# Row normalisation by the sum of absolute values: transfers moved to the software queue in a fixed order, each engine's share as a single packet

## The chip, the cores and the metric

The kernel runs on one core of one Trainium2 chip. The metric is the device time in microseconds (us). A ratio is the mean time of one kernel's fast runs over that of the other kernel's fast runs of the same rounds, so it is not quite the ratio of the medians that are quoted.

## The reference

```python
# x: (32, 512, 1024) float32
sums = np.sum(np.abs(x), axis=-1, keepdims=True)
return (x / (sums + 1e-8)).astype(np.float32)
```

That is 16,384 rows of 1,024 floats. 67.1 MB are read and 67.1 MB written.

## The kernel before

There are 8 tiles of 128 partitions x 16 rows x 1,024 floats, 8 MB each, and 3 buffers. Each tile is loaded by one transfer, worked on in place and stored, all on the hardware queue that SyncE issues. In the profiles DVE is VectorE, ACT is ScalarE, and Pool is GpSimd. DVE reduces the rows and takes the reciprocals. DVE then scales 10 of the 16 rows one by one, and ACT scales the other 6. The last two tiles are worked on and stored in chunks of 4 rows.

```python
def process_chunk(x_tile, out_ap, r0, rN, mv):
    s = stats.tile([P, rN], mybir.dt.float32, tag="s")
    nc.vector.tensor_reduce(out=s[:, :], in_=x_tile[:, r0 : r0 + rN, :], ...)   # cut: axis X, add, absolute value
    inv = stats.tile([P, rN], mybir.dt.float32, tag="inv")
    nc.vector.reciprocal(out=inv[:, :], in_=s[:, :])
    for r in range(rN):
        if r < mv:
            nc.vector.tensor_scalar_mul(...)        # cut: row r0 + r times inv[:, r]
        else:
            nc.scalar.activation(..., func=Copy, scale=inv[:, r : r + 1])
    nc.sync.dma_start(out=out_ap[:, r0 : r0 + rN, :], in_=x_tile[:, r0 : r0 + rN, :])

MV = 10
for i in range(ntiles):
    x_tile = sbuf.tile([P, R, d], x.dtype)          # R = 16, 3 buffers
    nc.sync.dma_start(out=x_tile[:, :, :], in_=x_t[i, :, :, :])
    if i < ntiles - 2:
        process_chunk(x_tile, out_t[i], 0, R, MV)
    else:
        C = 4
        for c0 in range(0, R, C):
            process_chunk(x_tile, out_t[i], c0, C, (MV * C) // R)
```

The compiler orders the instructions of each engine itself. On the queue the order became, with L for a load and S for a store: L0 L1 L2 S0 S1 S2 L3 L4 L5 S3 S4 S5 L6 L7, then S6 and S7 in four chunks each.

## Time and profile before

| | before |
|---|---|
| time, median of the first 3 runs | 318.28 us (318.22 to 318.55) |
| span of the profiled execution | 316.9 us |
| DVE busy / ACT busy | 60% / 18% |
| hardware queue, share of 16 engines' span | 98.6% |
| mean rate | 424 GB/s |

These lines are from the profile page of before: busy time by engine, the mean busy share of the 16 DMA engines in 40 slices of the span (in tenths), and the queue.

```profile
span 316.9 us, 261 instructions
...
DVE 190.8 (60%) x104; ACT 56.7 (18%) x53; POOL 0.2 (0%) x4
...
DMA  9999999999999999999999999999999999999797
...
q1 hardware_dynamic: 3168, 134.22, 98.6%
```

The DMA engines bound the kernel. They are busy in every slice, while DVE is idle 40% of the time. The view of waits gives DVE's idle time (line, what it waited for, us in total, times, longest):

```profile
DVE s L37 <- DMA x_tile<-in_x_dram: 111.2, 3, 44.6
```

DVE waits 111 us for loads, but the DMA engines are busy during those waits, with stores and then with the awaited loads, so this idle time costs nothing by itself.

The table of windows shows one place where the DMA engines do stop. The columns are the window, its length, busy time of DVE, ACT and POOL with instruction counts, the granted clock, the DMA share and GB/s.

```profile
286.00:293.00 7.00, 7.00 (x4) 2.19 (x2) 0.00 (x0) 1.00 1.01 433
293.00:295.00 2.00, 2.00 (x5) 0.85 (x1) 0.00 (x0) 1.00 0.58 246
295.00:299.00 4.00, 4.00 (x2) 3.41 (x4) 0.00 (x0) 1.00 1.00 422
299.00:301.00 2.00, 2.00 (x4) 0.00 (x0) 0.00 (x0) 1.00 0.62 262
```

At 294 and at 300 us the engines run dry, because DVE finishes the last tile's chunks late: it reduces the second chunk before it has scaled the first. Below, a stretch in which an engine has no packet to move is called a dry spot.

The trace also records every DMA packet, and when each of the 16 engines reports its share of a transfer as landed. From those records:

- A 64 KB packet takes 2.418 us at the median, which is 434 GB/s over 16 engines. An engine moves 8 such packets for an 8 MB transfer, 19.34 us.
- The records do not name the engine. I joined packets end to start into 16 chains. All figures "per engine" below are per chain.

### The profile page before, as it was taken

The numbers are of one execution on the slowest core, as the hardware profiler recorded it, in microseconds if no ns is written. First come the engines' busy times: TensorE is split into PE (matmuls) and PEld (weight loads), VectorE is DVE, ScalarE is ACT, GpSimd is POOL, SyncE is SP. The second block draws the span as 40 slices with busy tenths as digits, with TensorE's granted clock in tenths as the row PEclk, the third lists the DMA queues.
The fourth block names the chain that finished last, engine by engine and source line by source line (L and its number), as shares of the span: only waits on it lengthen the run. The fifth ranks groups of instructions, "written<-read, shape, count | busy, mean of one in ns | idle before, by whom it ended". The sixth has DMA issues, their size and how long they took to land.

```text
span 316.9 us, 261 instructions
## 1 busy us (share of the span) xinstructions
DVE 190.8 (60%) x104; ACT 56.7 (18%) x53; POOL 0.2 (0%) x4
## 2 busy tenths in 40 slices
DVE  0019999999990000039999999980000069999910
ACT  0010080080080000000160070080000002522520
POOL 0000000000000000000000000000000000000000
DMA  9999999999999999999999999999999999999797
GB/s 397 397 397 513 414 397 397 397 438 488 397 397 505 422 397 397 521 405 397 480 447 397 397 489 438 397 430 480 414 397 480 438 405 422 399 431 432 335 430 331
DMA packets 3170, 134.24 MB, mean 424 GB/s; under 512 B 352, under 2 KB 352, under 8 KB 352
## 3 DMA queue, kind: packets, MB, share of 16 engines
q1 hardware_dynamic: 3168, 134.22, 98.6%
q14 instruction: 2, 0.02, 0.0%
HBM read 67.11 MB, written 67.11 MB: 424 GB/s over the span
## 4 chain that ended last, share of the span: by engine, by line
DVE 57%; DMA 35%; issue 4%; ACT 0%; ACTq 0%; SPq 0%; DVEq 0%
DVE s L37 41%; DMA x_tile<-in_x_dram 35%; DVE x_tile L48 15%; DVE inv L45 1%; ACT x_tile L54 0%; ACTq L99 0%; SPq L60 0%; DVEq L45 0%; DVEq L48 0%
## 5 line engine op out<-in xcount | busy, mean ns | idle before, releaser
L37 DVE TENSOR_REDUCE s<-x_tile 128x4 f32<-128x4096 f32 (+1 forms) x14 | 138.3, 9891 | 111.2 <-DMA x_tile<-in_x_dram 111.2
L54 ACT ACTIVATE x_tile<-x_tile,inv 128x1024 f32<-128x1024 f32 x52 | 55.4, 1137 | 223.9 <-DVE inv L45 223.9
L48 DVE TENSOR_SCALAR x_tile<-x_tile,inv 128x1024 f32<-128x1024 f32 x76 | 51.4, 748 | 0.3
L54 ACT ACT_TABLE_LOAD x1 | 1.3, 1283 | 22.8 <-DMA x_tile<-in_x_dram 22.8
L45 DVE RECIPROCAL inv<-s 128x4 f32<-128x4 f32 (+1 forms) x14 | 2.6, 200 | 0.4
L88 POOL MEMSET const-bfloat16-1.0<- 128x1 bf16 x1 | 0.1, 101 | 0.0
L88 POOL MEMSET const-uint8-127<- 128x1 uint8 x1 | 0.1, 101 | 0.0
L88 POOL MEMSET const-float32-0.0<- 128x1 f32 x1 | 0.1, 98 | 0.2 <-issue 0.2
L88 POOL MEMSET const-float32-1.0<- 128x1 f32 x1 | 0.1, 98 | 0.0
## 6 DMA issues: line engine op xcount, KB each, us to landing
out_dram<-x_tile SPq DMA_DIRECT2D x8, 2048.0 KB, 9.9
x_tile<-in_x_dram SPq DMA_DIRECT2D x8, 51.0
out_dram<-x_tile SPq DMA_DIRECT2D x6, 29.5
```

Source lines behind the costliest of these rows:

```text
L37: nc.vector.tensor_reduce(out=s[:, :], in_=x_tile[:, r0 : r0 + rN, :], axis=mybir.AxisListType.X, op=mybir.AluOpType.add, apply_absolute_v ...
L45: nc.vector.reciprocal(out=inv[:, :], in_=s[:, :])
L48: nc.vector.tensor_scalar_mul(out=x_tile[:, r0 + r, :], in0=x_tile[:, r0 + r, :], scalar1=inv[:, r : r + 1],)
L54: nc.scalar.activation(out=x_tile[:, r0 + r, :], in_=x_tile[:, r0 + r, :], func=mybir.ActivationFunctionType.Copy, scale=inv[:, r : r + 1],)
L88: nc = _bacc.Bacc("TRN2", target_bir_lowering=False, num_devices=1)
```

## The change

The intent is to keep the DMA engines fed without a break. The first three loads stay on the hardware queue. Everything later goes to the software queue, which Pool issues, in one fixed order in which loads and stores alternate. Each engine's share of a transfer is asked for as a single packet. On the compute side, DVE scales half of the rows in one two-input multiply and ACT scales the other half, and only the last tile is split, into two halves.

```diff
+        nc.vector.tensor_scalar_add(out=s[:, :k], in0=s[:, :k], scalar1=EPS)
+        nc.vector.tensor_mul(out=x_tile[:, r0 : r0 + kv, :], in0=x_tile[:, r0 : r0 + kv, :],
+            in1=inv[:, :kv].unsqueeze(2).to_broadcast([P, kv, d]))          # kv = half of the rows
-            if r < mv:
-                nc.vector.tensor_scalar_mul(...)
 ...
+    def span(i):
+        k = R // 2 if i == ntiles - 1 else R
+        return [(r0, k) for r0 in range(0, R, k)]
 ...
+            (nc.sync if i < BUFS else nc.gpsimd).dma_start(
+                out=x_tile[:, r0 : r0 + k, :], in_=x_t[i][:, r0 : r0 + k, :], single_packet=True)
 ...
+            nc.gpsimd.dma_start(
+                out=out_t[i][:, r0 : r0 + k, :], in_=tiles[i][:, r0 : r0 + k, :], single_packet=True)
 ...
+    plan = [("L", i) for i in range(BUFS)]
+    for i in range(ntiles):
+        plan.append(("S", i))
+        nxt = i + BUFS - 1
+        if BUFS <= nxt < ntiles:
+            plan.append(("L", nxt))
+    last = max(k for k, p in enumerate(plan) if p[0] == "L")
+    plan[last - 1], plan[last] = plan[last], plan[last - 1]
+    with tc.manual_schedule():      # every engine keeps the program's order
 ...
```

The order is L0 L1 L2 S0 S1 L3 S2 L4 S3 L5 S4 L6 L7 S5 S6 S7, with L7 and S7 in two halves.

More of the change, by code (lines that the diff above doesn't have):

```diff
@@ L7 @@
 from concourse._compat import with_exitstack
+FP32 = mybir.dt.float32
+EPS = 1e-8
 @with_exitstack
@@ L26, with normalize @@
     ntiles = n // (P * R)
+    BUFS = 3
     x_t = x_flat.rearrange("(n p r) d -> n p r d", p=P, r=R)
     out_t = out_flat.rearrange("(n p r) d -> n p r d", p=P, r=R)
-    BUFS = 3
     sbuf = ctx.enter_context(tc.tile_pool(name="sbuf", bufs=BUFS))
-    stats = ctx.enter_context(tc.tile_pool(name="stats", bufs=BUFS))
-    def process_chunk(x_tile, out_ap, r0, rN, mv):
-        s = stats.tile([P, rN], mybir.dt.float32, tag="s")
+    stats = ctx.enter_context(tc.tile_pool(name="stats", bufs=4))
+    def normalize(x_tile, r0, k, kv):
+        s = stats.tile([P, R], FP32)
         nc.vector.tensor_reduce(
-            out=s[:, :],
-            in_=x_tile[:, r0 : r0 + rN, :],
+            out=s[:, :k],
+            in_=x_tile[:, r0 : r0 + k, :],
             axis=mybir.AxisListType.X,
@@ L43, in process_chunk @@
         )
-        inv = stats.tile([P, rN], mybir.dt.float32, tag="inv")
-        nc.vector.reciprocal(out=inv[:, :], in_=s[:, :])
-        for r in range(rN):
-            if r < mv:
-                nc.vector.tensor_scalar_mul(
-                    out=x_tile[:, r0 + r, :],
-                    in0=x_tile[:, r0 + r, :],
-                    scalar1=inv[:, r : r + 1],
-                )
-            else:
-                nc.scalar.activation(
-                    out=x_tile[:, r0 + r, :],
-                    in_=x_tile[:, r0 + r, :],
-                    func=mybir.ActivationFunctionType.Copy,
-                    scale=inv[:, r : r + 1],
-                )
@@ L60, in process_chunk @@
-        nc.sync.dma_start(out=out_ap[:, r0 : r0 + rN, :], in_=x_tile[:, r0 : r0 + rN, :])
-    MV = 10
-    for i in range(ntiles):
-        x_tile = sbuf.tile([P, R, d], x.dtype)
-        nc.sync.dma_start(out=x_tile[:, :, :], in_=x_t[i, :, :, :])
-        if i < ntiles - 2:
-            process_chunk(x_tile, out_t[i], 0, R, MV)
-        else:
-            C = 4
-            for c0 in range(0, R, C):
-                process_chunk(x_tile, out_t[i], c0, C, (MV * C) // R)
+        nc.vector.tensor_scalar_add(out=s[:, :k], in0=s[:, :k], scalar1=EPS)
@@ new lines, in normalize @@
+        inv = stats.tile([P, R], FP32)
+        nc.vector.reciprocal(out=inv[:, :k], in_=s[:, :k])
+        nc.vector.tensor_mul(
+            out=x_tile[:, r0 : r0 + kv, :],
+            in0=x_tile[:, r0 : r0 + kv, :],
+            in1=inv[:, :kv].unsqueeze(2).to_broadcast([P, kv, d]),
+        )
+        for r in range(kv, k):
+            row = x_tile[:, r0 + r, :]
+            nc.scalar.activation(
+                out=row,
+                in_=row,
+                func=mybir.ActivationFunctionType.Copy,
+                scale=inv[:, r : r + 1],
+            )
@@ new lines, in span, with load @@
+    def span(i):
+        k = R // 2 if i == ntiles - 1 else R
+        return [(r0, k) for r0 in range(0, R, k)]
+    tiles = {}
+    def load(i):
+        x_tile = sbuf.tile([P, R, d], FP32)
+        tiles[i] = x_tile
+        for r0, k in span(i):
+            (nc.sync if i < BUFS else nc.gpsimd).dma_start(
+                out=x_tile[:, r0 : r0 + k, :], in_=x_t[i][:, r0 : r0 + k, :], single_packet=True
+            )
+        for r0, k in span(i):
+            normalize(x_tile, r0, k, k // 2)
@@ new lines, in store @@
+    def store(i):
+        for r0, k in span(i):
+            nc.gpsimd.dma_start(
+                out=out_t[i][:, r0 : r0 + k, :], in_=tiles[i][:, r0 : r0 + k, :], single_packet=True
+            )
+    plan = [("L", i) for i in range(BUFS)]
[6 more added lines that the diff above has]
+    plan[last - 1], plan[last] = plan[last], plan[last - 1]
@@ L77 @@
+    with tc.manual_schedule():
+        for what, i in plan:
+            if what == "L":
+                load(i)
+            else:
+                store(i)
 _INS = ['x']
```

## The prediction

> **What bounds the kernel now.** The 16 DMA engines. The page's queue part gives the hardware queue 98.6% of 16 engines' span; its slices show DMA at 9 in 39 of 40; the mean is 424 GB/s. DVE is busy 60%, ACT 18%. The chain of waits names DVE reduces (41%), which misleads: DVE sits idle twice for about 44 us waiting for loads (timeline), but the DMA engines are writing stores then. All transfers run one after another on one queue. In the trace's DMA packets a 64 KB packet takes 2.418 us at the median, so an 8 MB transfer (8 per engine) takes 19.34 us, and transfers land 19.3 to 19.8 us apart: 434 GB/s. The Trainium skill ("DMA: Bandwidth & Descriptors", Where 436 GB/s comes from) puts the ceiling at 435; the trace agrees.
>
> **Where slack is left.** Sixteen transfers make 309.5 us. The rest of the 316.9 us span is about 2.9 us before the stream runs at rate, 0.9 us from the last landing to the end, and about 3.5 us of losses: roughly 1.2 us where load 2 meets store 0 (the packets at 58 us take 3.4 to 3.8 us), about 0.5 us at 236, and about 2 us near the end, where the engines run dry at 294 and 300 us because the last tile's chunks finish late on DVE.
>
> **What the change does.** Bytes, buffers and DMA engines stay. Per tile it adds a tiny add (about 0.2 us, like the reciprocal's 0.20) and multiplies 8 rows in one two-input instruction in place of 10 single-row ones (6.7 us). The reduce runs at 1.05 ns an element; the skill ("VectorE: DVE Perf Modes", The perf-mode tier table) gives fp32 tensor_tensor no faster mode, so I estimate 8192 x 1.05 = 8.6 us. DVE per tile goes from 24.2 to 26.3 us, ACT from 6 to 8 rows (8.5 us). Total DVE about 210 us, still far under 309.
>
> The order becomes L0 L1 L2 S0 S1 L3 S2 L4 S3 L5 S4 L6 L7 S5 S6 S7. Laying 19.34 us transfers against 26.3 us tiles, each transfer is issued before the engines run out: tightest is S1 (tile 1 done at about 75.5, S0 leaves the engines at about 80); all others have over 10 us of lead. Tile 7's halves are done at about 275 and 288 us, while S7 gets the engines only at 292 to 302. So the dry spots of the end go, worth about 2 us, and perhaps 1 us elsewhere. DVE's waits for loads (111 us) will shrink, but that is worth nothing: it is off the path. Single packets may save part of the 9 ns between 64 KB packets (2.418 against 2.409 at 435 GB/s), at most 1 us.
>
> **Sum.** 2.9 + 309.5 + 1 = 313.4 us span, plus the 1.4 us by which the measured time exceeds the span, plus about 0.7 us of mixed losses: **315.5 us**, 0.9% faster. 8 in 10: 312.5 to 321. Faster by over 2%: 0.08; within 2%: 0.76; slower by over 2%: 0.16.
>
> **What would show it.** DMA share 9 in all slices including the last, near 430 GB/s; 64 KB packets still about 2.42 us; two-input multiply 8.6 us; last store issued over 10 us before it begins to move.
>
> **What would make it wrong.** Slower: the software queue cuts descriptors smaller or feeds the engines more slowly (packet count or time per byte up), some engines lag, Pool's issues wait behind its in-order waits or behind DVE and the engines run dry, or loads and stores of the two queues meeting at 50 to 60 us cost more. Faster than 2% would need more than 435 GB/s, for which I see no room.

## The result, and the profile after

| | before | after |
|---|---|---|
| time, median of 6 runs | 318.26 us (317.98 to 318.55) | 318.21 us (317.48 to 318.75) |
| ratio | | 0.9996, 95% interval 0.9984 to 1.0007 |
| span of the profiled execution | 316.9 us | 316.6 us |

The time is the same. In a later batch (run e5 below), after took 319.97 us beside 318.55 for before, a ratio of 1.0041. Both ratios are well within 2% of 1.

The page of after, with the lines that answer to those of before, the multiply (line 50) and the software queue (q0):

```profile
span 316.6 us, 194 instructions
...
DVE 211.0 (67%) x36; ACT 68.8 (22%) x65; POOL 8.3 (3%) x19
...
DMA  9999999999999999999999999999999999999995
...
q0 software_dynamic: 2160, 109.05, 79.8%
q1 hardware_dynamic: 432, 25.17, 18.9%
...
L50 DVE TENSOR_TENSOR x_tile<-x_tile,inv 128x8192 f32<-128x8192 f32 (+1 forms) x9 | 69.7, 7744 | 0.6
```

The 7 of before in the slice from 293 to 301 us is a 9 now. The last slice is 5, in place of before's 7. In after's view of waits, DVE's time waiting for loads fell:

```profile
DVE s L40 <- DMA x_tile<-in_x_dram: 78.8, 5, 22.6
```

32 us less waiting on DVE bought no time. These lines of after's timeline are the issues of S1, of L3 and of the last store (start, duration, engine, line, operation, then the idle time before it and who ended it):

```profile
75.99 0.53 POOL L82 DMA_DIRECT2D out_dram<-x_tile  x1 [25.62 <-ACT x_tile L57]
...
82.20 0.54 POOL L74 DMA_DIRECT2D x_tile<-in_x_dram  x1 [5.68 <-DMA out_dram<-x_tile]
...
291.56 0.53 POOL L82 DMA_DIRECT2D out_dram<-x_tile  x1 [12.96 <-ACT x_tile L57]
```

S1 is issued at 75.99 us, while S0 lands at 81.5. The last store is issued at 291.56 and begins to move only at about 304. So the queue never emptied: the 16 chains of after show one gap of 0.3 us on one chain and no other dry time, where those of before average 1.7 us.

Where the gain went is seen when the span is cut at the landing records:

| us, profiled execution | before | after |
|---|---|---|
| first load has landed on the median engine | 22.24 | 22.23 |
| last store has landed on the median engine | 315.86 | 314.16 |
| last store has landed on the last engine | 315.96 | 315.20 |
| end of the span | 316.90 | 316.59 |

The median engine did finish 1.7 us earlier. But the last engine came 1.04 us after the median one in place of 0.10, and the span went on for 1.39 us after the last landing in place of 0.94. Of 1.7 us, 0.3 were left.

The landing records of the single transfers show where before's last engine caught up. It was 1.20 us behind the median one at the last landing before the first dry spot (295.58 against 294.38 us), 0.18 us at the next landing after it (300.43 against 300.26), and 0.10 at the end. In after it was 1.11 us behind at 257 us, and 1.04 at the end. So before had the same lateness, and its dry spots hid it.

### The profile page after: what moved, and what is told of

It reads as the page before. It is cut to its first block, busy times and chain, and to the rows that moved or that the text cites. A ratio compares the mean times of both kernels' runs of the same rounds, so it can differ in the third digit from the quotient of the medians.

```text
span 316.6 us, 194 instructions
## 1 busy us (share of the span) xinstructions
DVE 211.0 (67%) x36; ACT 68.8 (22%) x65; POOL 8.3 (3%) x19
## 4 chain that ended last, share of the span: by engine, by line
DVE 48%; DMA 35%; issue 4%; another core or an unknown queue 4%; POOLq 0%; POOL 0%; DVEq 0%
DMA x_tile<-in_x_dram 35%; DVE s L40 32%; DVE x_tile L50 15%; DVE inv L49 0%; DVE s L47 0%; POOLq L128 0%; POOL out_dram L82 0%; DVEq L50 0%; POOLq L82 0%
## 5 line engine op out<-in xcount | busy, mean ns | idle before, releaser
L40 DVE TENSOR_REDUCE s<-x_tile 128x16 f32<-128x16384 f32 (+1 forms) x9 | 137.9, 15320 | 78.8 <-DMA x_tile<-in_x_dram 78.8
L57 ACT ACTIVATE x_tile<-x_tile,inv 128x1024 f32<-128x1024 f32 x64 | 67.5, 1135 | 199.4 <-DVE inv L49 190.0
L50 DVE TENSOR_TENSOR x_tile<-x_tile,inv 128x8192 f32<-128x8192 f32 (+1 forms) x9 | 69.7, 7744 | 0.6
L82 POOL DMA_DIRECT2D out_dram<-x_tile x9 | 4.9, 547 | 247.5 <-DVE x_tile L50 183.0
L74 POOL DMA_DIRECT2D x_tile<-in_x_dram x6 | 3.2, 542 | 36.0 <-DMA out_dram<-x_tile 36.0
L49 DVE RECIPROCAL inv<-s 128x16 f32<-128x16 f32 (+1 forms) x9 | 2.2, 242 | 0.3
L47 DVE TENSOR_SCALAR s<-s 128x16 f32<-128x16 f32 (+1 forms) x9 | 1.6, 174 | 0.3
```

What stands on the lines that cost most here:

```text
L40: nc.vector.tensor_reduce(out=s[:, :k], in_=x_tile[:, r0 : r0 + k, :], axis=mybir.AxisListType.X, op=mybir.AluOpType.add, apply_absolute_v ...
L47: nc.vector.tensor_scalar_add(out=s[:, :k], in0=s[:, :k], scalar1=EPS)
L49: nc.vector.reciprocal(out=inv[:, :k], in_=s[:, :k])
L50: nc.vector.tensor_mul(out=x_tile[:, r0 : r0 + kv, :], in0=x_tile[:, r0 : r0 + kv, :], in1=inv[:, :kv].unsqueeze(2).to_broadcast([P, kv, d]),)
L57: nc.scalar.activation(out=row, in_=row, func=mybir.ActivationFunctionType.Copy, scale=inv[:, r : r + 1],)
L74: (nc.sync if i < BUFS else nc.gpsimd).dma_start(out=x_tile[:, r0 : r0 + k, :], in_=x_t[i][:, r0 : r0 + k, :], single_packet=True)
```

## The experiments

Theory A, formed from the table of landings: the DMA engines do not keep step, and a transfer ends with its last engine. The dry spots of before were time in which late engines caught up, so removing them was worth less than their average. Theory B, the rival: the removal is worth its full 1.8 us, and the software queue eats it. All kernels were run with 5 rounds beside before. All results were correct except where a wrong one is announced.

| run | transfers | turns from loads to stores | time, us (range) | before | ratio (95%) |
|---|---|---|---|---|---|
| e1 all hardware queue | after's order | 5 | 319.69 (318.22–320.05) | 318.75 | 1.0021 (1.0004–1.0038) |
| e2 no single packet | after's | 5 | 320.04 (318.76–320.86) | 318.75 | 1.0034 (1.0015–1.0053) |
| e3 DVE order pinned | before's | 3 | 317.47 (317.19–319.01) | 318.75 | 0.9966 (0.9949–0.9984) |
| e4 copy only | after's | 5 | 319.96 (319.86–320.18) | 318.75 | 1.0036 (1.0024–1.0048) |
| e5 after again | after's | 5 | 319.97 (318.51–320.65) | 318.55 | 1.0041 (1.0023–1.0059) |
| e6 early small store | before's | 3 | 317.98 (317.93–319.36) | 318.55 | 0.9987 (0.9973–1.0001) |
| e7 half tiles, alternating | finer, hardware | 10 | 320.10 (319.81–320.41) | 318.55 | 1.0046 (1.0034–1.0058) |
| e8 half tiles, grouped | grouped, hardware | 3 | 317.45 (317.19–317.51) | 318.55 | 0.9962 (0.9949–0.9974) |
| e9 e8 on the change's queues | grouped | 3 or more | 320.71 (320.32–321.85) | 318.50 | 1.0072 (1.0056–1.0087) |
| e10 e8 again | grouped, hardware | 3 | 317.28 (317.18–318.10) | 318.50 | 0.9967 (0.9955–0.9979) |
| e11 e8 all on the software queue | grouped | 3 | 321.62 (320.92–322.02) | 318.46 | 1.0099 (1.0086–1.0112) |
| e12 after all on the software queue | after's order | 5 | 319.97 (318.72–321.20) | 318.46 | 1.0047 (1.0026–1.0068) |

The same cuts of the span for the profiled execution of each (us). "Landed" is the median engine's last landing. "Late" is how much later the last engine's came. "End" is from there to the end of the span. One execution stands in each row, so "late" in particular varies from execution to execution.

| | landed | late | end | span |
|---|---|---|---|---|
| before | 315.86 | 0.10 | 0.94 | 316.9 |
| after | 314.16 | 1.04 | 1.39 | 316.6 |
| e1 | 314.38 | 2.57 | 0.92 | 317.9 |
| e2 | 314.20 | 2.73 | 1.39 | 318.3 |
| e3 | 313.98 | 2.31 | 0.94 | 317.2 |
| e4 | 314.84 | 1.93 | 1.37 | 318.1 |
| e5 | 314.53 | 2.08 | 1.39 | 318.0 |
| e6 | 314.01 | 1.26 | 0.89 | 316.2 |
| e7 | 315.52 | 2.16 | 0.92 | 318.6 |
| e8 | 313.90 | 0.87 | 0.92 | 315.7 |
| e9 | 314.84 | 2.14 | 1.94 | 318.9 |
| e10 | 313.83 | 1.05 | 0.93 | 315.8 |
| e11 | 315.62 | 1.33 | 2.51 | 319.5 |
| e12 | 315.11 | 0.72 | 1.48 | 317.3 |

### e1: the software queue undone

```diff
-            (nc.sync if i < BUFS else nc.gpsimd).dma_start(... single_packet=True)
+            nc.sync.dma_start(...)
-            nc.gpsimd.dma_start(... single_packet=True)
+            nc.sync.dma_start(...)
```

> The kernel after with every transfer on the hardware queue and no single packet; its fixed order and its compute are kept. Theory A (removing the dry spots is worth little, because the slowest DMA engine had only 0.65 us of them, and the engines then end up to 1.5 us apart): span about 316.0, the 0.4 us better than after only through a shorter end (0.95 us instead of 1.4 from the last landing to the end of the span); time about 317.5 to 318.0. Theory B (removing them is worth the full 1.8 us, and the software queue eats it): time about 316.3 to 316.8, a ratio of about 0.995 to the kernel before.

It took 319.69 us, slower than before (318.75). Theory B is refuted: without the software queue the gain did not appear. The end of the span did shorten to 0.92 us, as A expected, but the time missed A's number too, by 2 us. The last engine was 2.57 us late, more than in after's first trace. A alone does not say why engines fall further behind here.

### e2: the single packet dropped

```diff
-                ..., single_packet=True
```

> The kernel after with the single-packet request dropped, nothing else. In the trace of after the 64 KB packets of load 2 and store 0 alternate one by one from 57 us on although each share was asked for as a single packet. Theory A (the request changes nothing that the engines do at this size): same time as after within 0.3 us, 64 KB packets at 2.418 us, load 2 again lands at about 69.4 and store 0 at 81.5. Rival C (the request saves time between packets or keeps shares together): 1 us or more slower, or load 2 landing at another time.

Its ratio of 1.0034 has an interval that overlaps that of after (1.0041 in e5). The 64 KB packets again take 2.418 us. Load 2 landed at 69.3 and store 0 at 81.4 us, as in after (69.4 and 81.5). In both kernels the records show 64 KB packets of the two queues alternating one by one in that stretch. The request for a single packet changed nothing that can be seen.

### e3: only the dry spots taken from before

DVE is held to the program's order, so that each chunk is finished before the next one is reduced.

```diff
+    ctx.enter_context(tc.manual_schedule(engines={mybir.EngineType.DVE}))
     for i in range(ntiles):
```

> The kernel before with DVE's instructions in the program's order, nothing else: each 4-row chunk of the last two tiles is finished before the next is reduced, so that the first store of the last tile is issued at about 287 instead of 294 us. Both theories: the dry spots at 294 and 300 us go. Theory A: the slowest engine gains only its own dry time, span 0.6 to 0.9 us shorter (about 316.1), the engines' last packets spread over more than 1 us instead of 0.16. Theory B: 1.8 us shorter (about 315.1).

The windows of e3, the same ones as shown of before:

```profile
286.00:293.00 7.00, 6.83 (x6) 3.09 (x3) 0.00 (x0) 1.00 1.00 428
293.00:295.00 2.00, 2.00 (x2) 1.28 (x2) 0.00 (x0) 1.00 1.05 451
295.00:299.00 4.00, 3.86 (x4) 0.85 (x1) 0.00 (x0) 1.00 0.98 422
299.00:301.00 2.00, 2.00 (x2) 1.34 (x2) 0.00 (x0) 1.00 1.01 434
```

The DMA share at 293 to 295 us rose from 0.58 to 1.05, and at 299 to 301 from 0.62 to 1.01: the dry spots are gone. The median engine landed 1.9 us earlier, but the last one came 2.31 us after it, in place of 0.10. Over all runs 0.34% was gained, about 1.1 us by the ratio. (The traced execution was e3's slowest, 319.01 us. The others lie from 317.19 to 318.23.) A had expected a span 0.6 to 0.9 us shorter, B 1.8: the gain lies between them, nearer to A. So part of the dry time was indeed time in which late engines caught up. And removing it alone, with before's queue and before's order, does gain 1.1 us. Something in the change takes it back.

### e4: no compute (a wrong result)

```diff
-        for r0, k in span(i):
-            normalize(x_tile, r0, k, k // 2)
```

> The kernel after without its compute (wrong result on purpose: the output is the input). Stores can go as soon as a load has landed. Theory A (the DMA engines bound every stage, compute is off the path): span within 1 us of after's 316.6, 64 KB packets at 2.418 us. Rival D (waits for compute still cost DMA time somewhere): over 2 us shorter. Also: if the long packets (3.4 to 3.9 us on all 16 engines, at 58 us before and 53 us after) belong to the first store of the program, they move to where the first store is now, about 24 to 27 us; if they belong to the end of the three first loads, they stay near 55 to 60 us.

A pure copy in after's order and on after's queues takes 319.96 us. The full kernel took 319.97 in e5. It was run at another time. (A's expectation of a span within 1 us of 316.6 was missed: it was 318.1. After's own span was 318.0 in e5.) DVE's and ACT's work is off the path to within what can be measured. The long packets moved from 53 us to about 27 us, where the first store now begins, so they go with the first store.

The records of all six traces up to here showed one more thing. Packets that are too long lie near 117, 156, 195 and 255 us in the fixed order, and near 175 and 272 us in before's. These are the places where a load is followed by a store. There the last load packets take mostly 0.1 to 0.4 us longer on average, and up to 1.35 us longer on an engine that is already behind. The change turns from loads to stores 5 times, before 3 times. This is theory E. It names only one of the two directions. Some turns from stores to loads have long packets too: near 139 us in after, the first load packet after a store is 0.21 us too long on average, on all 16 engines, and the packet near 236 us in before lies at such a turn. After has 4 of these turns, before 2.

### e5: after again, on the chip of the second batch

> The kernel after, unchanged, on the chip of this batch, so that the others have it beside them; the last batch ran on a chip where before took 318.75 and after was not run. Theory E, formed from the last batch: each switch of the DMA engines from loads to stores lengthens the last load packets before it, by 0.1 to 0.3 us on average and by up to 1.3 us on one or two engines that are already behind; after has 5 such switches, before 3; and after has no dry spot at the end in which the late engines catch up. So: 318.2 to 320.0 us, slower than or equal to before, the slowest engine ending 1 to 3 us behind the median one.

It came out as expected: 0.41% slower than before, where the first batch had shown no difference (0.9984 to 1.0007). Why the two batches differ stays open. Its runs spread over 2.1 us, those of before over 0.7. The last engine was 2.08 us late.

### e6: a small store at the very start

```diff
+    w = stats.tile([P, 128], x.dtype, tag="w")
+    nc.gpsimd.memset(w[:, :], 0.0)
+    nc.scalar.dma_start(out=out_t[0][:, 0, 0:128], in_=w[:, :])
```

(added to e3)

> The kernel of the pinned DVE order plus a store of zeros, 512 bytes a row, into the first rows of the output at the very start, which the real store later overwrites. In the copy run the long packets (1.2 us too long on all engines) moved with the first store, from 53 to about 27 us. If that is a cost of the first store of a program, it should now fall into the first 2 us, where the engines wait for the first load's data anyway, and the long packets at 58 us should be gone: time 0.8 to 1.2 us under the pinned order's 317.5, about 316.4. If it belongs to the first time that a long stream of loads turns into stores, the packets at 58 us stay and the time is that of the pinned order.

The packets at 58 us stayed 1.15 us too long on average, and nothing was gained. A first store as such is not what costs. In e8 and e10, with 32 KB packets, the same place costs 0.6 us. What it is stays open. It is the same in before and after (1.23 and 1.24 us), so the change does not touch it.

### e7 and e8: the same half tiles, with 10 and with 3 turns

Both are e1 with `R = 8` and `BUFS = 6`. e7 keeps the alternating plan. e8 replaces it:

```diff
-    plan = [("L", i) for i in range(BUFS)] ...          # the alternating plan
+    plan = []
+    for g in range(0, ntiles, BUFS):
+        group = range(g, min(g + BUFS, ntiles))
+        plan += [("L", i) for i in group] + [("S", i) for i in group]
```

> The all-hardware-queue kernel with tiles of 8 rows in place of 16 and 6 buffers in place of 3 (same bytes, same SBUF), in the same alternating fixed order: 10 switches from loads to stores in place of 5. Theory E (switches cost): packets longer than normal add up to 3.5 to 5 us per engine instead of 2.6 to 3.1, time 320.5 to 323. Rival F (late engines arise by time or by chip, not by switches): same as the all-hardware-queue kernel, 318 to 320.

> The same tiles of 8 rows and 6 buffers, but six loads, then six stores, then six loads, and so on: 3 switches. Theory E: packets longer than normal add up to about 2.2 us per engine as in the pinned DVE order, time 317 to 318, 3 us or more under the alternating one. Rival F: equal to the alternating one within 0.5 us.

These two differ in the order of the same transfers and in nothing else, and they differ by 2.65 us (320.10 and 317.45). The windows of e7, then of e8, over the stretch in which e7 alternates:

```profile
60.00:110.00 50.00, 47.24 (x16) 17.06 (x16) 0.00 (x0) 1.00 0.99 425
110.00:160.00 50.00, 36.51 (x12) 9.01 (x9) 0.00 (x0) 1.00 1.00 430
160.00:235.00 75.00, 48.96 (x14) 16.59 (x16) 0.00 (x0) 1.00 1.00 424
```

```profile
60.00:110.00 50.00, 33.80 (x12) 12.79 (x12) 0.00 (x0) 1.00 0.99 428
110.00:160.00 50.00, 29.69 (x9) 8.53 (x8) 0.00 (x0) 1.00 1.00 432
160.00:235.00 75.00, 50.77 (x16) 17.07 (x16) 0.00 (x0) 1.00 1.00 433
```

The DMA engines are equally busy (0.99 to 1.00) but move less in e7: 424 against 433 GB/s in the last window. That is the mark of longer packets, not of waiting. By the records, the packets of an engine take 4.52 us more in e7 than 2.418 us per 64 KB, and 2.84 us more in e8. About 1.2 us of both comes from the smaller packets as such. The median engine landed 1.6 us later in e7 and its last engine was 1.3 us further behind. That lateness grew only while e7 alternated: 0.21 us at 62 us, 2.15 at 228, where the alternation ends, and 2.16 at the end. In e8 it was 0.23 at 62 us, 0.28 at 198 and 0.87 at the end.

F is refuted, and theory E holds in this: alternating the same transfers costs time, as longer packets and a later last engine. A turn costs about 2.65 / 7 = 0.4 us here, as an estimate from the difference of 7 turns in each direction; these two runs can't tell the directions apart. A fixed price per turn is not shown. At e8's two later turns the packets are hardly longer (under 0.04 us on average), and from e1 to e7, with 5 more turns and smaller packets, the ratio to before rises only from 1.0021 to 1.0046, about 0.8 us. E's numbers were missed, too: e7 took 0.4 us less than its range, and the difference is 2.65 us where 3 or more were expected.

e8 also beats before, by 0.38%. Its five runs lie within 0.32 us of each other.

### e9 and e10: the change's queues under the grouped order

e9 is e8 with the first six loads on the hardware queue, everything later on the software queue, and single packets. e10 is e8 unchanged.

> The half-tile grouped kernel with the queues of the change: the first six loads on the hardware queue, everything later on the software queue as single packets. Theory E plus a fixed end cost (1.38 us from the last landing to the end of the span where the software queue is used, 0.92 where it is not): 0.5 us slower than the grouped kernel on the hardware queue, about 317.95, still faster than before. Rival G (the software queue itself, not the order, makes after slow): 319 us or more.

> The half-tile grouped kernel on the hardware queue once more, beside the other one on the same chip: 317.4 to 317.6, 0.3 to 0.4% under before, if the gain is of the kernel and not of one batch.

e10 repeated e8. e9 missed by far: 320.71 us in place of 317.95, which is 3.4 us above e10. The trace had a long stretch, about 33 to 92 us, in which loads of one queue and stores of the other alternate packet by packet, and one engine landed 2.3 us behind the median one with the first store. I took that mixing for the cause and tried it.

### e11 and e12: no two queues at once

```diff
-            (nc.sync if i < BUFS else nc.gpsimd).dma_start(
+            nc.gpsimd.dma_start(
```

(in e9 for e11, in after for e12)

> The half-tile grouped kernel with every transfer on the software queue as single packets, the first loads too, so that no two queues are ever active. The run before had loads on the hardware queue and stores on the software queue alternating packet by packet from 33 to 98 us and took 320.71, not the 317.95 expected. If the mixing of the two queues is what cost (many more turns between loads and stores, and one engine 2 us behind from 51 us on): no mixing, the slowest engine ends near 314.5 to 315, the end costs 1.4 to 1.9 us, time 317.7 to 318.6. If the software queue costs by itself: 320 or more.

> The kernel after with the first three loads on the software queue too: no stretch of 12 us in which load 2 and store 0 alternate. In after that stretch is short, so if only mixing and turns matter: between 0.5 us faster and 0.5 us slower than after (the first load can start a little later, up to 0.5 us), 319.5 to 320.4 on this chip, with load 2 landing at about 62 instead of 69.4. If the first loads on the hardware queue are worth something by an early start: 1 us or more slower than after.

e11 took 321.62 us, still more than e9. So mixing is not needed for the loss: the software queue with single packets costs when it carries many transfers. (That the single packets as such cost nothing was tested in e2, with 64 KB packets, and not with the 32 KB packets of e9 and e11.) Against e8's traced execution, e11's span is 3.76 us longer. The first load lands 0.79 us later, the rest of the stream takes 0.93 us longer, the last engine is 0.46 us later, and the end takes 1.59 us longer. The end grows with the number of transfers on the software queue: 0.92 us with none (e8), 1.39 with 15 (after), 1.48 with 18 (e12), 1.94 with 28 (e9) and 2.51 with 34 (e11). In after, with 15 transfers, the queue's share is small: e5's ratio of 1.0041 and e1's of 1.0021 have overlapping intervals. e12 equals after, so the three first loads on the hardware queue, and the 12 us in which the two queues mix, cost and gain nothing that can be measured. Why the rest of e11's stream is slower stays open.

## Why the prediction was right or wrong

**Right.**

- The DMA engines bound every stage (e4: a copy takes the same time).
- The multiply took 8.69 us (estimate 8.6), from the rate of the reduce and what the Trainium skill ("VectorE: DVE Perf Modes", The perf-mode tier table) says of two-input fp32 instructions; the trace bears it out.
- The tightest transfer was S1 and no transfer came late. The dry spots went. The 32 us less of DVE waiting were worth nothing.
- 318.21 us lies inside the range of 312.5 to 321, and the change stayed within 2%. Two of the signs that I had named did not show: the last slice of DMA is 5 and not 9, and the mean rate is 424 GB/s as before, not near 430.

**Wrong.** The forecast of 315.5 us, 0.9% faster, was 2.7 us too low. The measured change is nil, or a slight loss on the second batch. Here are the terms of the sum, and one that it lacked, against the traced execution of after, which took 318.36 us. The 2.9 us is the first load's landing less 19.34 us, the 309.5 us is 128 packets of 2.418 us, and the mixed losses are what then remains up to the median engine's last landing:

| term, us | predicted | measured |
|---|---|---|
| until the stream runs at rate | 2.9 | 2.9 |
| 16 transfers | 309.5 | 309.5 |
| mixed losses (long packets) | 0.7 | 1.77 |
| last engine behind the median | not in the sum | 1.04 |
| last landing to the end of the span | 1.0 | 1.39 |
| beyond the span | 1.4 | 1.76 |

- **The step that failed is "So the dry spots of the end go, worth about 2 us, and perhaps 1 us elsewhere".** The dry spots did go, and they were worth 1.7 us on the median engine. But a store has landed only when its last engine has. In before the first dry spot let the last engine catch up, from 1.20 us behind the median one to 0.18. In after nothing did, and the last engine ended 1.04 us behind. So the last engine, which sets the end, gained only 0.76 us (315.96 to 315.20). e3 shows it apart from all else: over its runs, removing the dry spots gained 1.1 us. In its traced execution, the slowest, the median engine lands 1.9 us earlier, the last one 2.31 us behind it.
- **The "perhaps 1 us elsewhere" was not gained.** The sum let the mixed losses fall to 0.7 us, and they stayed at 1.77. The same subtraction gives 1.73 for before (315.86 less 2.90, 309.50 and 1.73 of dry time). The new order turns the engines from loads to stores 5 times in place of 3, and I gave a turn no cost. I had even seen the long packets at 58 and 236 us, and did not ask whether more turns would bring more of them. e7 against e8 shows the cost of turns: 2.65 us for 7 more in each direction. e1 shows that after's order and compute, on before's queue, do not gain, and e3 that before's order does. They lie about 1.75 us apart by their ratios. Two more turns at 0.4 us would explain 0.8 of it; the rest is not explained.
- **The end.** I took 0.9 to 1.0 us over from before. With 15 transfers on the software queue it is 1.39.
- **Single packets** were to save up to 1 us. They saved none (2.418 us per 64 KB with and without).
- **Beyond the span.** I subtracted one execution's span from another's median. In the traced executions, where both are known, the difference is 1.76 to 1.95 us.

The rivals that I had named for "slower" were partly at work elsewhere. The software queue with single packets costs 3.4 to 4.2 us where it carries 28 to 34 transfers (e9 and e11 over e10 and e8), but little where it carries 15.

It stays open why it is mostly one or two engines that fall behind, and by how much in a given execution. Also open are what lengthens a packet at a turn, why some turns cost nearly nothing, and the 1.2 us at the first long store.

## What to carry to other kernels

When the DMA engines are busy all through, compute the floor from the duration of one packet, and then look at what lies above it engine by engine, since an average over 16 engines hides the last one, which sets the end. Keep loads with loads and stores with stores in groups as large as the buffers allow: the same transfers took 317.45 us in groups of six and 320.10 in alternation. A small dry spot near the end may be partly useful time in which late engines catch up, so removing it is worth less than it measures, and e3's one-line pin of DVE's order (0.34%) did more than the whole change.

## What the Trainium skill lacked or had wrong

- "DMA: Bandwidth & Descriptors", Queues, rings and completion order, says that an engine drains a whole packet of a queue's ring, typically 9 to 17 descriptors, before it switches to another queue. Here, with single packets asked for and without, the two queues alternated after every 64 KB record of the trace (from 57 to 69 us in after and in e2). The trace does not say whether such a record is a packet of the ring or one descriptor, so either the page does not hold here or each share was cut into packets of one record, although a single packet had been asked for in after.
- The same page has nothing on turns between loads and stores. Here 7 more turns in each direction with the same transfers cost 2.65 us (e7 against e8), and single load packets before a turn took up to 1.35 us longer on an engine that was behind.
- The ceiling of 435 GB/s that the same page, Where 436 GB/s comes from, works out holds here: 434 GB/s at 2.418 us per 64 KB packet. The page has no measured time of such packets. Here 32 KB packets take 1.213 us, 8 ns more per 64 KB, so that smaller packets cost e8 about 1 us per engine (128 times 8 ns).
- The same page, Latency and other measured facts, gives about 0.6 us to the first byte on the hardware path and about 1 us on the software path. The difference agrees: e12's first load was issued 0.52 us later than after's (1.26 against 0.74) and landed 0.95 us later, which leaves 0.43 us. No page gives the cost of the software queue at the end of a kernel, from the last landing to the end of the span, which here grew from 0.92 us without the software queue to 2.51 us with 34 transfers on it.
- No page that I read gives an amount by which the 16 engines drift apart in a long stream. Here the last engine landed 0.7 to 2.7 us after the median one, and 0.10 us in the one kernel that ran dry shortly before its end.
